# Modulation steps handed out one at a time inside the first filter units, with later norms, in a two-layer mLSTM / Hyena / neighbourhood-attention trunk

## The chip, the core and the metric

One NeuronCore of a Trainium2 chip runs the whole forward pass in one launch. The metric is device time in microseconds; smaller is better. Its engines are named here as the profile names them: PE is TensorE (matrix products; PEld is its weight load), DVE is VectorE, ACT is ScalarE, POOL is GpSimd and SP is SyncE, which issues most transfers. Each engine works off its own instructions strictly in order, and engines wait for one another by semaphores.

## The reference, cut to what matters

A stream of 1024 latent tokens and one of 256 context tokens, 1024 channels wide, pass two layers. Layer 0 mixes an mLSTM (four heads) with a Hyena long convolution; layer 1 is neighbourhood attention with 16 heads. Each layer ends in a squared-ReLU MLP. What the change touches is the start of layer 0: the modulation, the first norm, and the filters of the Hyena, which do not depend on the tokens.

```python
mod_x = (silu_c @ w_mod[l] + b_mod[l])[:, None, :]        # shift, scale, gate
hx = rms_norm(x) * (1.0 + sc1) + sh1
...
h = jnp.sin(freq * (emb @ w1 + b1))
h = jnp.sin(freq * (h @ w2 + b2))
h = (h @ w3).astype(f32).reshape(L, HYENA_ORDER, 2, MIX_B)
h = h * jnp.exp(-t * deltas)[:, None, None, :]
h = h * lax.rsqrt(jnp.sum(h * h, axis=0, keepdims=True) + EPS)
```

Every `rsqrt` of the kernel (the token norms, the norms of q and k in the attention, the norms of the mLSTM heads and of the filters) is computed on ACT as `Exp(-0.5 * Ln(v))` with one Newton step on DVE behind it.

## The kernel before, in words

Tokens stand transposed, 128 channels by 512 tokens to a tile, in three groups (512, 512 and 256 tokens, `GR`). A product of full precision is made of three passes with split operands (L177 to L179 for the projections, L312 to L314 for the second half of the MLP). Program order and priorities go into a scheduler, which writes the final order of each engine; it is that order which the chip runs.

The stages, in order: (1) filters: `filter_hidden` makes the two small sine layers, and nine turns of a loop run `filter_taps` for one of eight units (taps L514 and L515, norm `newton_small` L140 and L141, scaling by the result L525, transposes L532) and `filter_spectrum` for the unit before. Between them the callback `between` places the modulation of layer 0 (`mod_part`, L218) and the norms of the three token groups (`norm_sum` with L252, `rstd_from` with L132 and L133, `norm_apply` with L289); (2) the Hyena blocks with projections as filler, and the gates (`Ln` and `Exp` at L691 and L732); (3) four mLSTM heads (`Ln` and `Exp` at L799 and L800, head norm at L140 and L141, its result transposed at L872); (4) output projection and norm; (5) the MLP of layer 0, with the norm of layer 1 at its end; (6) eight pairs of attention heads, in which `natten_proj` norms two groups of q and three of k (square L900, sum L902, then L904, `Ln` L905, `Exp` L906) while `natten_attn` of the pair before runs (scores L978 and L979, `Exp` L989 and L990, transposes L999, their copies L1001 out of the only buffer `psm`); (7) the output projection, a norm and the second MLP.

ACT evaluates `Sin`, `Ln` and `Exp` from tables, and an instruction ACT_TABLE_LOAD brings in a set of them when the next function is in another set than the one that is loaded. A pass over the finished order puts these loads in; the kernel's own part in it is one line behind the sine layers, at the end of the modulation:

```python
between(-1)
tc.keep_in_program_order(S.preload_act_table_set("natural_log_exp_and_others"))
```

It is L559 before and L563 in the changed kernel. The set that it names holds both `Ln` and `Exp`: in the order before, no load stands behind it, though `Ln` and `Exp` alternate to the end.

Of the kernel before, what the change touches and what calls it, by code (L numbers as in the profile page):

```python
# [17 lines left out]
P = 128  # L18
LAT, CTX, NT = 1024, 256, 1280
# [8 lines left out]
def kernel(ctx: ExitStack, tc: tile.TileContext, A, out):  # L28
    nc = tc.nc
# [9 lines left out]
    def mk(pool, shape, tag, bufs, dt=F32):  # L39
        cnt[0] += 1  # L40
        return pool.tile(shape, dt, tag=tag, bufs=bufs, name=f"{tag}_{cnt[0]}")
# [4 lines left out]
    OR = ((2, 0), (0, 0), (2, 1), (0, 1), (2, 2), (1, 0), (1, 1), (1, 2))  # L46
    E1, E2, E3, E4, E5 = None, None, None, None, None
    NHT, NQ = 1, 2
    NS, NA = (0, 2, 5), {0: (0, 0), 0.5: (0, 8)}
    PN = "n"  # L50
    TA, TB, TC, TV, PO = "m", "m", "m", "m", "f"
    ONP0 = ()
# [23 lines left out]
    def pt(shape, tag):  # L76
        cnt[0] += 1
        return psp[0].tile(shape, F32, tag=tag, bufs=psp[1][tag], name=f"ps{tag}_{cnt[0]}")
# [22 lines left out]
    def sub(o, a, b):  # L101
        return tt(o, a, b, ALU.subtract)

    def mul(o, a, b):
        return tt(o, a, b, ALU.mult)
# [102 lines left out]
    def mod_steps(l, g, pool, bufs, tag):  # L208

        ps = [None]  # L210
        for i in range(16):
            def step(k=i % 8, c0=i // 8 * 256):
                if k == 0 and c0 == 0:
                    ps[0] = pt([P, 512], tag)
                w = mk(pool, [P, 8, P], bufs[0], bufs[1]).rearrange("p (j a) b -> p j (a b)", j=4)
                nc.sync.dma_start(w, A["w_mod"][l, k * P:(k + 1) * P, g * 2048:(g + 1) * 2048].rearrange("p (j c) -> p j c", j=4)[:, :, c0:c0 + 256])
                for j in range(4):
                    T.matmul(ps[0][32 * j:32 * j + 32, c0:c0 + 256], sil[:, k, :], w[:, j], start=(k == 0), stop=(k == 7))  # L218
                if k == 7 and c0:
                    mod_end(l, g, ps[0], tag)  # L220
            yield step

    def mod_part(l, g, pool, bufs, tag="g"):
        for f in mod_steps(l, g, pool, bufs, tag):
            f()
# [268 lines left out]
                sub(st[64:128, t], h[r], st[64:128, t].bitcast(F32))  # L494
        return st

    def filter_taps(qd, o, h2, dec, fa, fp):

        w3 = mk(fa, [64, 256], "w3", 1)
        nc.scalar.dma_start(w3, A["f_w3"][:, o, qd].rearrange("p d c -> p (d c)"))  # L500
        w3h = mk(fa, [P, 256], "w3h", 2, F32R)
        w3l = mk(fa, [P, 256], "w3l", 2, F32R)
        G.memset(w3l[64:128].bitcast(F32), 0.0)
        dsk = mk(fa, [1, P], "dsk", 2)
        nc.scalar.dma_start(dsk, A["hy_d"][:, o, qd])
        S.copy(w3h[0:64], w3)
        S.copy(w3h[64:128], w3)
        sub(w3l[0:64], w3, w3h[0:64].bitcast(F32))
        hT = mk(fp, [P, 2, NT], "hT", NHT)
        ss = mk(fp, [P, 4, 2, 3], "ss", 2)  # L510
        for d in range(2):
            for g, (c0, n) in enumerate(GR):
                ps = pt([P, 512], "t")
                T.matmul(ps[:, :n], w3h[:, d * P:(d + 1) * P], h2[:, c0:c0 + n], start=True, stop=False)  # L514
                T.matmul(ps[:, :n], w3l[:, d * P:(d + 1) * P], h2[:, c0:c0 + n], start=False, stop=True)  # L515
                mul(hT[:, d, c0:c0 + n], ps[:, :n], dec[:, c0:c0 + n])
                sq = mk(fp, [P, 512], "sq", 1)
                S.activation(sq[:, :n], hT[:, d, c0:c0 + n], AF.Square, accum_out=ss[:, 0, d, g:g + 1])
        v, r, tmp = [ss[:, i, :, 0:2] for i in (1, 2, 3)]
        add(ss[:, 0, :, 1:2], ss[:, 0, :, 0:1], ss[:, 0, :, 1:2])  # L520
        V.tensor_scalar(out=v, in0=ss[:, 0, :, 1:3], scalar1=EPS, scalar2=None, op0=ALU.add)
        newton_small(v, r, tmp)
        for d in range(2):
            for l, (a, b) in enumerate(((0, LAT), (LAT, NT))):
                S.activation(hT[:, d, a:b], hT[:, d, a:b], AF.Copy, scale=r[:, d, l:l + 1])  # L525
        hfb = mk(fp, [P, 10, 2, P], "hfb", 2)
        for pr in range(5):
            ps = pt([P, 2, 2, P], "t")
            for i in range(2):
                s = 2 * pr + i  # L530
                for d in range(2):
                    T.transpose(ps[:, i, d], hT[:, d, s * P:(s + 1) * P], ident)  # L532
            S.copy(hfb[:, 2 * pr:2 * pr + 2], ps)
        for s in (0, 8):
            add(hfb[0:1, s, 0], hfb[0:1, s, 0], dsk)
        return hfb
# [14 lines left out]
        X = dft_fwd(mm, fp, False)  # L551
        nc.sync.dma_start(Gd[o, qd], X)

    def filters(hc, Gd, between):
        with tc.tile_pool(name="fa", bufs=1) as fa:
            with tc.tile_pool(name="hid", bufs=1) as hid:
                h2 = filter_hidden(hid, fa)
                between(-1)
                tc.keep_in_program_order(S.preload_act_table_set("natural_log_exp_and_others"))  # L559
            with tc.tile_pool(name="fp", bufs=1, reuse_waits="tile") as fp:  # L560
                last = None
                for u in range(9):
                    if u < 8:  # L563
                        qd, o = divmod(u, 2)
                        if o == 0:
                            dec = mk(fa, [P, NT], "dec", 1)
                            nc.scalar.dma_start(dec, A["dec"][qd])
                        hfb = filter_taps(qd, o, h2, dec, fa, fp)
                        if u == 0:
                            tS = mk(fa, [P, 10, P], "tS", 1)  # L570
                            nc.scalar.dma_start(tS, A["tabF"][:, 2])
                        between(u - 1.5)
                    if last is not None:
                        filter_spectrum(*last, hc, tS, fp, Gd)
                        between(u - 1)
                    last = (qd, o, hfb)
# [447 lines left out]
    Gd = dram([2, 4, P, 2, 10, P])  # L1024
# [30 lines left out]
    with tc.tile_pool(name="hp", bufs=1, side="right") as hp:  # L1055
        hc = {}
        stage = lambda: mk(hp, [P, 512], "st", 1)
        with tc.tile_pool(name="mo", bufs=1, side="right") as mo:

            def xload(t0, n):  # L1060
                t_ = {}

                def f(k):
                    if k % 2 == 0:
                        t_[k // 2] = mk(mo, [P, 2, 512], "wm", 3)
                        nc.sync.dma_start(t_[k // 2][:, :, :n], A["xT"][:, k:k + 2, t0:t0 + n])
                    return t_[k // 2][:, k % 2, :n]
                return f

            norms = {}  # L1070

            def between(u):
                if u == -1:
                    hc.update(hyena_consts(hp))
                    mod_part(0, 0, mo, ("wm", 3), "q")
                for v in NS:
                    g = NS.index(v)
                    t0, n = GR[g]
                    which = 0 if t0 < LAT else 1
                    if u == v:  # L1080
                        norms[g] = norm_sum(xload(t0, n), n, False), xload(t0, n)
                    if u in (v, v + 0.5):
                        r, x = norms[g]
                        norm_apply(r, x, n, 0, 0, which, h[0][g], h[1][g], False, range(0, 8)[slice(*NA[u - v])])
                if u > 4 and u == int(u):
                    filler(FS[u - 5], stage)

            filters(hc, Gd, between)
        open_w()
        psum(**PS1)  # L1090
        with tc.tile_pool(name="wp2", bufs=1, reuse_waits="tile") as wp:
            hc["tI"] = mk(wp, [P, 2, 10, P], "tI", 1)
            nc.scalar.dma_start(hc["tI"], A["tabI"])
            u = decimate(hy_block(0, h, hc, wp), wp)
            for qd in range(4):
                if qd == GQ:
                    gs = gates(h, wp, gk)
                B = hyena_fft(qd, 0, u, hc, wp, Gd)
                if qd == GQ - 0.3:
                    gs = gates(h, wp, gk)  # L1100
                x1 = decimate(hy_block(3 * qd + 1, h, hc, wp), wp)
                x2 = hy_block(3 * qd + 2, h, hc, wp)
                filler(FH[2 * qd], stage)
                z = hyena_gate(qd, 0, B, x1, x2, hc, wp, mixd)
                B = hyena_fft(qd, 1, z, hc, wp, Gd)
                if qd < 3:
                    u = decimate(hy_block(3 * qd + 3, h, hc, wp), wp)
                filler(FH[2 * qd + 1], stage)
                if qd == GQ - 0.5:
                    gs = gates(h, wp, gk)  # L1110
                hyena_gate(qd, 1, B, x1, x2, hc, wp, mixd)
    psum(**PS3)
    with tc.tile_pool(name="gp", bufs=1, reuse_waits="tile", side="right") as gp:
        cst = mlstm_consts(gp)
        with tc.tile_pool(name="ml", bufs=1, reuse_waits="tile") as ml:
            h2 = []
# [68 lines left out]
    with tc.tile_pool(name="nl", bufs=1, reuse_waits="tile") as nl, \  # L1185
# [13 lines left out]
        h2 = new_h(LG)  # L1199
# [168 lines left out]
```

## Time and profile before

| | us |
|---|---|
| three timed runs, median | 3416.87 |
| lowest and highest | 3413.32, 3423.29 |
| the profiled execution's own time | 3412.15 |
| its span in the trace | 3410.4 |
| PE busy | 3256.5 (95%) |
| DVE busy | 2056.0 (60%) |
| ACT busy | 1211.5 (36%) |
| mean granted clock of TensorE | 0.983 of full |

Busy time is summed over the span; an engine with a small share can still be the one that another waits for in some stage. In the rows of the trace a number like 0.63 behind a start time is the duration in us, and what stands in square brackets is how long the engine sat idle before it and what ended that wait.

### The profile page before, as it was taken

To read this page: it belongs to the slowest core of one execution; us is meant where nothing else is said; L and a number is where in the kernel's file an instruction comes from. 1 tells how busy PE (TensorE), PEld (TensorE's weight loads), DVE (VectorE), ACT (ScalarE), POOL (GpSimd) and SP (SyncE) were. 2 spreads that over 40 slices of the span, in tenths; PEclk is the share of its full clock that TensorE was granted. 3 is DMA by queue.
4 is the path that set the end of the run, shared out by engine and by line. 5 is a ranking of instruction groups with operands and counts; after the bars stand their busy time and mean duration, and the time that the engine had idled before them with its cause. 6 is when DMAs were issued, how large, how long until landed. Compare 5 with 4: busy or idle time off the path is not lost.

```text
span 3410.4 us, 45323 instructions
## 1 busy us (share of the span) xinstructions
PE 3256.5 (95%) x18044; PEld 2652.5 (78%) x18044; DVE 2056.0 (60%) x3655; ACT 1211.5 (36%) x2555; POOL 355.8 (10%) x295
## 2 busy tenths in 40 slices
PE   6889989999989999999999999999999899999999
PEld 4777878777877888788888777777777688888887
DVE  4858979366576445444454776666666755545444
ACT  5742222244343121211111476666665421111111
POOL 0341232101120000000000211111110200000000
PEclk8999999999999999999999999999999999999999
DMA  6432211775632121212111212221224211111111
GB/s 210 151 110 66 72 64 64 256 233 198 204 126 87 61 82 56 93 56 87 56 37 38 78 47 72 69 67 62 70 78 161 68 56 47 47 50 47 47 50 68
DMA packets 140878, 306.12 MB, mean 90 GB/s; under 512 B 12497, under 2 KB 74057, under 8 KB 139258
## 3 DMA queue, kind: packets, MB, share of 16 engines
q1 hardware_dynamic: 131018, 266.60, 23.8%
q0 software_dynamic: 6464, 28.84, 2.8%
q10 hardware_dynamic: 3184, 7.78, 0.7%
q8 instruction: 142, 2.33, 0.3%
q14 instruction: 70, 0.57, 0.1%
HBM read 255.93 MB, written 43.05 MB: 88 GB/s over the span
## 4 chain that ended last, share of the span: by engine, by line
PE 64%; DVE 5%; DMA 4%; ACT 3%; issue 1%; POOL 0%; ACTq 0%; SPq 0%; DVEq 0%; POOLq 0%
PE psg L177 10%; PE psg L178 10%; PE psg L179 10%; PE psf L312 8%; PE psf L313 8%; PE psf L314 8%; DMA wm<-in_w_mod 2%; PE psf L1014 2%; PE psm L999 1%; DVE n L108 1%; PE psf L978 1%; PE psf L979 1%; PE psf L1018 1%; PE psm L1006 1%; DVE h L108 1%
## 5 line engine op out<-in xcount | busy, mean ns | idle before, releaser
L177 PE MATMUL psg<-h,wh 128*128 128x512 f32 (+1 forms) x2728 | 1017.6, 373 | 16.7 <-ACT h L289 8.3
L179 PE MATMUL psg<-h,wl 128*128 128x512 f32 (+1 forms) x2728 | 1009.2, 370 | 10.8 <-POOL wl L113 6.0
L178 PE MATMUL psg<-h,wh 128*128 128x512 f32 (+1 forms) x2728 | 1014.8, 372 | 4.2 <-DVE h L108 3.0
L177 PEld LDWEIGHTS psg<-h,wh 128*128 128x128 f32 x2728 | 518.8, 190 | 111.3 <-issue 16.2
L178 PEld LDWEIGHTS psg<-h,wh 128*128 128x128 f32 x2728 | 519.4, 190 | 100.7 <-issue 14.0
L179 PEld LDWEIGHTS psg<-h,wl 128*128 128x128 f32 x2728 | 518.9, 190 | 101.3 <-issue 10.8
L108 DVE SCALAR_TENSOR_TENSOR x<-psf,modT,x 128x512 f32<-128x512 f32 (+1 forms) x512 | 347.4, 683 | 225.6 <-PE psf L314 225.4
L313 PE MATMUL psf<-al,w2h 128*128 128x512 f32 (+1 forms) x1280 | 473.3, 370 | 0.3 <-DVE al L113 0.3
L314 PE MATMUL psf<-ah,w2l 128*128 128x512 f32 (+1 forms) x1280 | 472.2, 369 | 0.0
L312 PE MATMUL psf<-ah,w2h 128*128 128x512 f32 (+1 forms) x1280 | 470.6, 370 | 0.9 <-ACT ah L112 0.8
L112 ACT CAST w2h<-w2r 128x1024 fp32r<-128x1024 f32 x64 | 67.3, 1052 | 765.8 <-PE psf L313 594.8
L312 PEld LDWEIGHTS psf<-ah,w2h 128*128 128x128 f32 x1280 | 241.7, 189 | 44.5 <-ACT ah L112 3.2
L313 PEld LDWEIGHTS psf<-al,w2h 128*128 128x128 f32 x1280 | 242.0, 189 | 42.1 <-DVE al L113 1.4
L314 PEld LDWEIGHTS psf<-ah,w2l 128*128 128x128 f32 x1280 | 242.0, 189 | 41.3 <-issue 1.2
L112 ACT CAST wh<-wr 128x1024 fp32r<-128x1024 f32 (+2 forms) x144 | 148.6, 1032 | 288.1 <-PE psg L178 225.2
L113 DVE TENSOR_TENSOR wl<-wr,wh 128x1024 fp32r<-128x1024 f32 (+1 forms) x105 | 127.5, 1214 | 151.3 <-ACT wh L112 150.9
L108 DVE SCALAR_TENSOR_TENSOR rr<-psg,rr 128x512 f32<-128x512 f32 x160 | 101.4, 634 | 179.6 <-ACT rr L301 179.6
L113 POOL TENSOR_TENSOR wl<-wr,wh 128x1024 fp32r<-128x1024 f32 (+1 forms) x39 | 134.0, 3436 | 607.2 <-ACT wh L112 554.9
L113 DVE TENSOR_TENSOR w2l<-w2r,w2h 128x1024 fp32r<-128x1024 f32 x64 | 78.3, 1223 | 153.1 <-ACT w2h L112 151.3
L301 ACT ACTIVATE rr<-psg 128x512 f32<-128x512 f32 x160 | 88.1, 551 | 196.6 <-PE psg L179 195.3
L112 ACT CAST ah<-rr 128x512 fp32r<-128x512 f32 x160 | 92.4, 578 | 168.1 <-DVE rr L108 168.1
L113 DVE TENSOR_TENSOR al<-rr,ah 128x512 fp32r<-128x512 f32 x160 | 101.8, 637 | 80.5 <-ACT ah L112 80.3
(295 smaller groups left out, 4329.7 us busy)
## 6 DMA issues: line engine op xcount, KB each, us to landing
wm<-in_w_mod SPq DMA_DIRECT2D x96, 512.0 KB
wr<-in_w SPq DMA_DIRECT2D x64, 512.0 KB
w2r<-in_w SPq DMA_DIRECT2D x64, 512.0 KB
big<-d SPq DMA_DIRECT2D x39, 640.0 KB
TM<-in_rpbT POOLq DMA_DIRECT2D x64, 384.0 KB, 3.4
wr<-in_w_in SPq DMA_DIRECT2D x29, 512.0 KB
wr<-in_w_qkv SPq DMA_DIRECT2D x24, 512.0 KB
d<-b SPq DMA_DIRECT2D x8, 1280.0 KB
```

The lines of the kernel that those rows point to most:

```text
L108: return V.scalar_tensor_tensor(out=o, in0=a, scalar=s, in1=b, op0=op0, op1=op1)
L112: S.copy(hi, x)
L113: (e or V).tensor_tensor(out=lo, in0=x, in1=hi.bitcast(F32), op=ALU.subtract)
L177: T.matmul(ps[:M, :n], hi[:, k, :M], hh[g][:, k, :n], start=(i == 0), stop=False)
L178: T.matmul(ps[:M, :n], hi[:, k, :M], hl[g][:, k, :n], start=False, stop=False)
L179: T.matmul(ps[:M, :n], lo[:, k, :M], hh[g][:, k, :n], start=False, stop=(i == len(ks) - 1))
L301: S.activation(r[:, :n], ps[:, :n], AF.Relu)
L312: T.matmul(ps[:, :n], w2h[:, d], ah[g], start=(i == 0), stop=False)
L313: T.matmul(ps[:, :n], w2h[:, d], al[g], start=False, stop=False)
L314: T.matmul(ps[:, :n], w2l[:, d], ah[g], start=False, stop=(i == 1))
L978: T.matmul(o, Q[hh][:, c0:c0 + P], kx, start=True, stop=False)
L1014: T.matmul(po[64 * hh:64 * hh + 64, rb], Vw[:, rb + j, 64 * hh:64 * hh + 64], pT[hh][0][rb][:, j], start=(j == 0), stop=False)
```

## The change

`mod_part` is no longer run in one go at `between(-1)`. Its sixteen steps (one load of 512 KB by SP and four matrix products each) go into a list, and `filter_taps` takes one from it after each of its six products with `h2` and after each of its five transposes. The norms of the first two token groups begin one unit later (`NS`), and before a norm is applied all steps that are left are taken. The ring `wm` has five buffers in place of three. The load of `dec` for the first quarter is issued ahead of the sine layers.

```diff
-    NS, NA = (0, 2, 5), {0: (0, 0), 0.5: (0, 8)}
+    NS, NA = (1, 3, 5), {0: (0, 0), 0.5: (0, 8)}
...
                 S.activation(sq[:, :n], hT[:, d, c0:c0 + n], AF.Square, accum_out=ss[:, 0, d, g:g + 1])
+                tick()
...
             S.copy(hfb[:, 2 * pr:2 * pr + 2], ps)
+            tick()
...
         with tc.tile_pool(name="fa", bufs=1) as fa:
+            dec = mk(fa, [P, NT], "dec", 1)
+            nc.scalar.dma_start(dec, A["dec"][0])
             with tc.tile_pool(name="hid", bufs=1) as hid:
...
-                        t_[k // 2] = mk(mo, [P, 2, 512], "wm", 3)
+                        t_[k // 2] = mk(mo, [P, 2, 512], "wm", 5)
...
+            def tick(n=1):
+                for f in mods[:n]:
+                    f()
+                del mods[:n]
...
                     hc.update(hyena_consts(hp))
-                    mod_part(0, 0, mo, ("wm", 3), "q")
+                    mods.extend(mod_steps(0, 0, mo, ("wm", 5), "q"))
...
                     if u in (v, v + 0.5):
+                        tick(16)
```

What the scheduler makes of it is shown at three places. Lines of the changed kernel are higher by 4 in the attention and by 1 to 10 elsewhere. On PE, at the start of the program, the sixteen steps (L218) stood among the sine layers (L482) and the first taps (L514, L515) already. Before:

```order
L480 MATMUL psf_130<-emb_113,fw_12_115 64x320 x2
L218 MATMUL psq_173<-wm_174,sil 32x256 x4
...
L218 MATMUL psq_173<-wm_198,sil 32x256 x4
L482 MATMUL psf_144<-fh_19_134,fw_13_117 64x320 x2
L482 MATMUL psf_148<-fh_19_134,fw_13_117 64x320 x2
L218 MATMUL psq_173<-wm_204,sil 32x256 x4
...
L218 MATMUL psq_173<-wm_234,sil 32x256 x4
L514 MATMUL pst_301<-h2s_161,w3h_291 128x512
```

And now:

```order
L480 MATMUL psf_132<-emb_115,fw_13_117 64x320 x2
L218 MATMUL psq_198<-wm_199,sil 32x256 x4
...
L218 MATMUL psq_198<-wm_259,sil 32x256 x4
L482 MATMUL psf_146<-fh_20_136,fw_14_119 64x320 x2
L482 MATMUL psf_150<-fh_20_136,fw_14_119 64x320 x2
L218 MATMUL psq_198<-wm_283,sil 32x256 x4
...
L218 MATMUL psq_198<-wm_331,sil 32x256 x4
L218 MATMUL psq_198<-wm_359,sil 32x256
L514 MATMUL pst_192<-h2s_163,w3h_182 128x512
```

Five steps stood ahead of the second sine layer and six stand there now; eleven stood ahead of the first taps, and eleven and a quarter do now. On ACT, the first three dozen rows: where the line of the preload went. Before it stood behind the copy of the finished modulation (L229):

```order
L352 DMA cb_171<-in_conv_b 128x12
L567 DMA dec_287<-in_dec 128x1280
L500 DMA w_50_289<-in_f_w 64x256
...
L456 ACT_TABLE_LOAD
L456 ACTIVATE fh_19_134<-fx_125 128x640
...
L140 ACT_TABLE_LOAD
L140 ACTIVATE ss_300<-ss_300 128x2x2
L229 COPY n_47_270<-psq_173 128x512
L559 ACT_TABLE_LOAD
L141 ACTIVATE ss_300<-ss_300 128x2x2
```

Now it stands ahead of the first sine (L456), whose own load comes after it:

```order
L352 DMA cb_173<-in_conv_b 128x12
L563 ACT_TABLE_LOAD
L500 DMA w_31_180<-in_f_w 64x256
...
L456 ACT_TABLE_LOAD
L456 ACTIVATE fh_20_136<-fx_127 128x640
...
L140 ACT_TABLE_LOAD
L140 ACTIVATE ss_191<-ss_191 128x2x2
L229 COPY n_89_413<-psq_198 128x512
L141 ACT_TABLE_LOAD
L141 ACTIVATE ss_191<-ss_191 128x2x2
```

What was a load by name at L559 is a load ahead of the `Exp` at L141, and from there on each `Ln` and the next `Exp` have a load of their own. The third place is ACT in the attention, at the second of the five norms of a pair of heads, the one at 2125 us of the trace. Before:

```order
L904 ACTIVATE n_3100_17619<-psn_17621,epsc 128x512
L905 ACTIVATE n_3102_17623<-n_3100_17619 128x512
L906 ACTIVATE n_3102_17623<-n_3102_17623 128x512
L1001 COPY s_3046_17369<-psm_17365 128x384
L1001 COPY s_3048_17375<-psm_17371 128x384
```

And now:

```order
L908 ACTIVATE n_3100_17619<-psn_17621,epsc 128x512
L909 ACT_TABLE_LOAD
L909 ACTIVATE n_3102_17623<-n_3100_17619 128x512
L910 ACT_TABLE_LOAD
L910 ACTIVATE n_3102_17623<-n_3102_17623 128x512
L1005 COPY s_3046_17369<-psm_17365 128x384
L1005 COPY s_3048_17375<-psm_17371 128x384
```

Two loads came in and nothing else moved. Over the whole program ACT has 2143 rows before and 2278 now, and 4 table loads before against 139: 12 each at L140 and L141, 11 each at L132 and L133, 40 at L909 and 39 at L910, 4 each at L803 and L804, and one each at L203, L456, L563, L695, L736 and L993. Behind the filters, the gates and the first Hyena blocks the orders of PE, DVE, ACT and POOL are the same but for these loads.

More of the change, by code (lines that the diff above doesn't have):

```diff
@@ L495, in filter_hidden, with filter_taps @@
         return st
-    def filter_taps(qd, o, h2, dec, fa, fp):
+    def filter_taps(qd, o, h2, dec, fa, fp, tick):
         w3 = mk(fa, [64, 256], "w3", 1)
@@ L552, in filter_spectrum, with filters @@
         nc.sync.dma_start(Gd[o, qd], X)
-    def filters(hc, Gd, between):
+    def filters(hc, Gd, between, tick):
         with tc.tile_pool(name="fa", bufs=1) as fa:
+            dec = mk(fa, [P, NT], "dec", 1)
+            nc.scalar.dma_start(dec, A["dec"][0])
             with tc.tile_pool(name="hid", bufs=1) as hid:
@@ L564, in filters @@
                         qd, o = divmod(u, 2)
-                        if o == 0:
+                        if o == 0 and qd:
                             dec = mk(fa, [P, NT], "dec", 1)
                             nc.scalar.dma_start(dec, A["dec"][qd])
-                        hfb = filter_taps(qd, o, h2, dec, fa, fp)
+                        hfb = filter_taps(qd, o, h2, dec, fa, fp, tick)
                         if u == 0:
@@ L1068, in xload @@
                 return f
-            norms = {}
+            norms, mods = {}, []
+            def tick(n=1):
+                for f in mods[:n]:
+                    f()
+                del mods[:n]
             def between(u):
@@ L1086, in between @@
                     filler(FS[u - 5], stage)
-            filters(hc, Gd, between)
+            filters(hc, Gd, between, tick)
         open_w()
```

## Prediction

> **What bounds the kernel now.** I read the page first, then the busy time by stretches, the groups of ACT, and the timelines of the places where a load is added. The page's first part says which engine is full:
>
> ```profile
> PE 3256.5 (95%) x18044; PEld 2652.5 (78%) x18044; DVE 2056.0 (60%) x3655; ACT 1211.5 (36%) x2555; POOL 355.8 (10%) x295
> ```
>
> TensorE (PE) bounds the whole, and ACT is idle for two thirds. But that is a mean. The stretches, with start and end, length, then busy time of PE, PEld, DVE, ACT and POOL, granted clock, DMA share and GB/s, show the start, the filters, the mLSTM heads, the norms ahead of the first MLP, and the attention:
>
> ```profile
> 0.00:50.00 50.00, 27.45 (x164) 9.33 (x165) 16.65 (x40) 21.91 (x41) 1.64 (x9) 0.85 0.85 271
> 42.00:250.00 208.00, 176.83 (x1115) 146.17 (x1116) 140.38 (x304) 133.32 (x290) 66.89 (x63) 0.93 0.40 135
> 640.00:960.00 320.00, 310.21 (x1936) 253.44 (x1935) 193.34 (x451) 130.15 (x394) 38.91 (x18) 0.99 0.63 209
> 960.00:1060.00 100.00, 87.78 (x393) 65.68 (x392) 78.28 (x112) 44.33 (x75) 26.57 (x19) 0.93 0.31 108
> 1975.00:2570.00 595.00, 583.73 (x3827) 456.45 (x3826) 411.23 (x912) 397.45 (x975) 88.51 (x132) 1.00 0.23 71
> ```
>
> In the first 50 us PE idles for 22.55 us; in the filters no engine is full, so a chain through several of them sets the pace; in the attention PE is at 98% and ACT at 67%.
>
> **What the order did with the change.** The steps of the modulation were spread among the sine layers and the first taps before, and they still are, at nearly the same places. What moved in earnest is one line on ACT: the load of the set that holds both `Ln` and `Exp` now runs ahead of the sine, whose own load discards it. From then on each `Ln` and each `Exp` behind it fetches its set: 139 loads where 4 were. One of the new ones (L563) runs ahead of the first sine, where ACT is waiting anyway; 134 others are new. The groups give counts and places, and the load's time:
>
> ```profile
> L132 ACT ACTIVATE n<-n 128x512 f32<-128x512 f32 (+1 forms) x11 | 6.3, 577 | 0.3
> L140 ACT ACTIVATE ss<-ss 128x4 f32<-128x4 f32 (+1 forms) x12 | 2.4, 203 | 3.7 <-DVE ss L521 3.0 <-DVE ss L866 0.7
> L799 ACT ACTIVATE big<-big 128x1280 f32<-128x1280 f32 x4 | 5.1, 1275 | 3.7 <-DVE big L798 3.7
> L905 ACT ACTIVATE n<-n 128x512 f32<-128x512 f32 (+1 forms) x40 | 23.7, 593 | 2.0 <-DVE n L108 1.2
> L140 ACT ACT_TABLE_LOAD x1 | 1.3, 1283 | 0.0
> ```
>
> A load took 1283 ns, so a pair of `Ln` and `Exp` costs ACT 2.57 us more, and all 134 cost 171.9 us. The two loads that before has inside the filters show that nothing else is paid:
>
> ```profile
> 42.85 1.28 ACT L140 ACT_TABLE_LOAD   x1
> 44.14 0.21 ACT L140 ACTIVATE ss<-ss 128x4 f32<-128x4 f32 x1
> 44.26 0.57 ACT L229 COPY n<-psq 128x512 f32<-128x512 f32 x1
> 44.84 1.28 ACT L559 ACT_TABLE_LOAD   x1
> 46.13 0.21 ACT L141 ACTIVATE ss<-ss 128x4 f32<-128x4 f32 x1
> ```
>
> The copy ends at 44.83 and the load starts at 44.84; the next function starts 0.01 us after the load's end. The Trainium skill, ScalarE: Activation LUTs, section "What ACT_TABLE_LOAD costs", gives 1283 ns for the load, which the trace shows, and about 1380 ns for a drain with it, 2.66 us for every switch, which these rows do not show. By that page the 134 would cost ACT 356 us, and the sum at the end, its stalls grown by 2.66 to 1.28, would be near 3725.
>
> **What lies on the path, stage by stage.** Attention first: 80 of the loads (40 at L909, 39 at L910, one at L993), 102.6 us, ten to each of eight pairs of heads. Three of the five norms of one pair of heads, ACT's rows and the PE row that comes next:
>
> ```profile
> 2105.93 0.63 ACT L906 ACTIVATE n<-n 128x512 f32<-128x512 f32 x1
> 2107.25 0.46 ACT L1001 COPY s<-psm 128x384 f32<-128x384 f32 x1
> 2107.76 0.55 PE L999 MATMUL psm<-ident,pe 128*128 128x128 f32 x3
> ...
> 2125.99 0.64 ACT L906 ACTIVATE n<-n 128x512 f32<-128x512 f32 x1
> 2127.25 0.48 ACT L1001 COPY s<-psm 128x384 f32<-128x384 f32 x1 [0.63 <-PE psm L999]
> 2127.79 0.55 PE L999 MATMUL psm<-ident,pe 128*128 128x128 f32 x3
> ...
> 2141.45 0.63 ACT L906 ACTIVATE n<-n 128x512 f32<-128x512 f32 x1
> 2142.75 0.60 ACT L900 ACTIVATE n<-psg 128x512 f32<-128x512 f32 x1 [0.67 <-PE psg L179]
> 2143.55 1.02 PE L902 MATMUL psn<-n,bd 128*128 128x512 f32 x2
> ...
> 2156.26 0.83 ACT L938 CAST KK<-n 64x256 fp32r<-64x256 f32 x2 [1.87 <-DVE n L96]
> 2157.17 0.39 PE L978 MATMUL psf<-KK,Q 128*128 128x256 f32 x1
> ```
>
> The next transposes need the copy, since `psm` is one buffer. In the first case the copy ends at 2107.71, 0.05 ahead of PE, and ACT has hardly a gap between: PE is late by some 2.4 us. In the second ACT has 0.63 of idle and PE a margin of 0.06: 2.57 - 0.69 = 1.9 us. In the first k norm the square L900 waits 0.67, so PE's sum is late by 1.9 again. The other two k norms follow within 12 us, and the last cast ends at 2157.09, 0.08 ahead of the scores L978, behind `Exp`, DVE and cast in a row; of the three pairs' 7.70 us I take 6.4, between 1.9 (the first alone) and 7.0 (all but 0.67). Together 10.7 us of 12.83 to a pair of heads, 86 us to eight; bounds 50 (the three readings alone) and 102.6. PE has no slack to hide it, having idled 11.3 of 595 us.
>
> The filters: eight norms at L140 and L141 and three at L132 and L133 lie there, 22 loads, of which two were paid before: 20, 25.7 us. The second unit shows the chain:
>
> ```profile
> 64.00 0.21 ACT L140 ACTIVATE ss<-ss 128x4 f32<-128x4 f32 x1
> 64.67 0.21 ACT L141 ACTIVATE ss<-ss 128x4 f32<-128x4 f32 x1
> 67.54 2.99 ACT L525 ACTIVATE hT<-hT,ss 128x1024 f32<-128x1024 f32 x4 [2.67 <-DVE ss L108]
> 68.74 0.44 PE L532 MATMUL pst<-ident,hT 128*128 128x128 f32 x2
> ```
>
> The scaling waits for DVE, which needs L141; the transposes follow. I take 22 us, bounds 10 and 25.7. Gates and heads hold 18 loads, 23.1 us. The four head norms are exposed, as PE already waits for their product, while the loads at L803 and L804 lie beside a PE that is 97% busy; I take 9, bounds 0 and 23. The eight norms left (three ahead of each MLP's first products or at layer 0's end, two in layer 1) are 20.5 us; the last of a stage is awaited in full, the others run beside products of another group: 15, bounds 7 and 20.5. The rows for these:
>
> ```profile
> 774.03 0.66 PE L872 MATMUL psm<-ident,big 128*128 128x128 f32 x4 [1.66 <-DVE big L96]
> 1043.92 0.38 PE L177 MATMUL psg<-h,wh 128*128 128x256 f32 x1 [1.61 <-ACT h L289]
> ```
>
> Sum of the loads: 86 + 22 + 9 + 15 = 132 us.
>
> **The clock.** Each such stall can also cost speed afterwards. A stretch of 3.41 us in which PE idled, and the next one; then products at half and at full clock:
>
> ```profile
> 915.95:919.36 3.41, 1.56 (x12) 1.23 (x11) 3.41 (x5) 2.06 (x7) 0.00 (x0) 1.00 0.22 78
> 919.36:922.77 3.41, 3.41 (x14) 3.12 (x14) 3.41 (x6) 1.81 (x5) 0.61 (x1) 0.50 0.56 180
> ```
>
> ```profile
> 2667.16 0.63 PE L177 MATMUL psg<-h,wh 128*128 128x512 f32 x1
> 2670.15 0.52 PE L178 MATMUL psg<-h,wh 128*128 128x512 f32 x1
> 2670.50 0.39 PE L179 MATMUL psg<-h,wl 128*128 128x512 f32 x1
> 2673.03 0.39 PE L178 MATMUL psg<-h,wh 128*128 128x512 f32 x1
> ```
>
> 1.85 us idle in one stretch, and the next has a granted clock of 0.50. From 2667.16 to 2670.15 seven products start, 0.43 us each; from 2670.50 to 2673.03 eleven, 0.23 each. A half-speed stretch thus does 8 products in place of 14.8 and loses 1.6 us. New stalls of 1.8 us or more: four to each of eight pairs of heads, and about 22 elsewhere. One of 1.9 lies within a single stretch in (3.41 - 1.9)/3.41, nearly half, of the cases, one of 2.4 gives 1.85 us to one stretch in about 0.6 of them, the last of the pair always. I count 17 in the attention (one lost time falls into a later stall) and 8 elsewhere: 25 x 1.6 = 40 us, bounds 0 and 54 x 1.6 = 86. The Trainium skill, TensorE: Matmul & The Clock Gate, Part 1, has the clock fall after at least one idle window of about 3.4 us; the row above fell after 1.85. By that page the stalls here would leave the clock alone, and the sum would be 3547 (the first rival).
>
> **The start.** Sixteen loads of 512 KB feed the modulation, and PE waits for them:
>
> ```profile
> PE psq L218 <- DMA wm<-in_w_mod: 16.2, 10, 4.3
> ```
>
> With five buffers the loads queue without gaps; the first row by stretches has DMA at 0.85, so at most 0.15 x 50 = 7.5 us are to be had. But unit 0 hangs on the sine layers, whose second one now stands behind one step more. I take 2 us of gain, between 7 and a loss of 3. SP's queue has the same sixteen loads first; those of `xT` behind them keep their places but for their turn with the stores of the spectra, so the norms that are asked for a unit later start where they did, and the last one was not moved. The load of `dec` that goes ahead on ACT's queue costs nothing, since ACT idles until the first sine layer's products. POOL's order is the same.
>
> **Sum.** The profiled execution's time is 3412.15 us (span 3410.4). 132 + 40 - 2 = 170 gives 3582 us. The median of the runs is 4.7 us above it, so I forecast 3587.
>
> **The rivals.** First, the clock stays: the loads stall PE, but stalls of 1.9 to 4.5 us, cut up by the sequence of other products, do not throttle: 3587 - 40 = 3547 us. For it: PE is busy on both sides of each stall, and the clock answers a stretch's mean. Against it: the row at 915.95. Second, each load costs as much again, since ACT must run empty ahead of it: the stalls double, and nearly every one then fills a stretch (60 us of clock), 3417 + 264 + 60 - 2 = 3739. Against it: the rows at 44.26 to 46.13. This is the drain that the Trainium skill names in the section cited above. Third, the loads are hidden: ACT has 198 us of idle in the attention and needs 103 of it, so if PE's queue ran ahead only the filters would pay, 3417 + 22 - 2 = 3437. Against it: margins of 0.05 and 0.06 us. Fourth, on the other side, faster: the load at L563 serves the whole program, so that `Ln` and `Exp` find what they need and the loads listed are not carried out, and the deeper ring saves 7 us by the DMA's share, or at best the 16.2 us that PE waits for these loads: 3410 to 3401. It decides if the profile after shows four or five loads. Against it: the trace before has the four loads that its order lists, each carried out in 1283 ns.
>
> **Chances.** The forecast 0.62, by itself 3560 to 3645. Clock unmoved 0.24. Drain 0.05. Hidden 0.05. Faster 0.04. The range 3525 to 3645 takes in the first two, with the loads at 108 us and no throttling below, and at 170 us and 60 of throttling above. About 0.3% (10 us) is what a measurement of this kernel tells from no change. Faster 0.03, within it 0.02, slower 0.95.
>
> **What would show it.** Right: 139 ACT_TABLE_LOAD in the groups of ACT at about 1283 ns, ACT busy near 1385 us; the attention, 595 us before, near 708; L999, L902 and L978 waiting 2 us and more behind ACT; granted clock there near 0.96. Wrong: an attention of less than 640 us, or new waits in the filters alone. If the clock stays at 1.00 in the attention, the first rival was right.

## The result and the profile after

The changed kernel took 3584.34 us (median of 6 runs, 3580.29 to 3591.22) where the kernel before took 3418.30 (6 runs, 3413.32 to 3423.96): 1.0486 times as long, with a 95% interval of 1.0473 to 1.0499. The forecast was 3587. The profiled execution took 3585.11 us, with a span of 3583.3 and a mean granted clock of 0.969, where before had 3410.4 and 0.983.

The busy times of the changed kernel, from its page:

```profile
PE 3308.9 (92%) x18044; PEld 2689.1 (75%) x18044; DVE 2052.9 (57%) x3655; ACT 1383.4 (39%) x2690; POOL 339.4 (9%) x295
```

Two things are to be seen. ACT has 171.9 us more than before; the 135 loads that came in are 135 x 1.283 = 173.2 us, so its other work is 1.3 us shorter. And the span splits: it is 172.9 us longer, PE is busy 52.4 us longer with the same 18044 products, and idle 120.5 us longer (3583.3 - 3308.9 against 3410.4 - 3256.5). Idle time is waiting. Products that take longer are products at a lower clock, and the clock's own record agrees: what was not granted is (1 - 0.969) x 3583.3 = 111.1 us against (1 - 0.983) x 3410.4 = 58.0, so 53.1 us more.

The groups of ACT show the loads; 102 of the 139 are in these rows, the others at L133, L141, L803, L804 and six single lines:

```profile
L909 ACT ACT_TABLE_LOAD x40 | 51.3, 1283 | 1.5 <-DVE n L108 0.8
L910 ACT ACT_TABLE_LOAD x39 | 50.0, 1283 | 0.7
L140 ACT ACT_TABLE_LOAD x12 | 15.4, 1283 | 0.3
L132 ACT ACT_TABLE_LOAD x11 | 14.1, 1283 | 0.2
```

To see where the time went, both spans are cut at the same instructions: the last product of the filters, the first of the mLSTM heads, the first of the output projection, the first of the second half of the MLP, the first sum of a q or k norm (L902, now L906), and the last score (L978, now L982). The columns are start and end, length, then busy time of PE, PEld, DVE, ACT and POOL, granted clock, DMA share and GB/s. The kernel before:

```profile
0.00:206.58 206.58, 164.12 (x1091) 126.96 (x1092) 141.99 (x311) 134.24 (x295) 54.46 (x57) 0.93 0.50 165
206.58:637.57 430.99, 382.72 (x2195) 327.59 (x2194) 321.45 (x576) 101.15 (x179) 99.35 (x33) 0.94 0.28 90
637.57:958.27 320.70, 310.91 (x1950) 254.43 (x1948) 192.28 (x449) 130.01 (x394) 38.43 (x17) 0.99 0.64 210
958.27:1008.86 50.59, 43.51 (x196) 33.94 (x194) 39.61 (x55) 24.57 (x38) 16.35 (x9) 0.93 0.51 179
1008.86:1981.29 972.43, 952.58 (x5081) 786.93 (x5081) 503.83 (x749) 218.30 (x356) 40.29 (x34) 0.99 0.20 64
1981.29:2613.58 632.29, 619.18 (x4090) 483.97 (x4091) 441.24 (x986) 418.64 (x1036) 88.36 (x134) 1.00 0.24 76
2613.58:3410.37 796.79, 783.46 (x3449) 638.68 (x3447) 415.65 (x533) 184.55 (x260) 18.51 (x12) 1.00 0.17 58
```

The changed kernel:

```profile
0.00:234.81 234.81, 174.21 (x1092) 131.68 (x1092) 141.46 (x312) 162.28 (x316) 49.51 (x57) 0.90 0.43 143
234.81:664.44 429.63, 383.66 (x2195) 328.34 (x2194) 321.35 (x576) 103.45 (x181) 90.28 (x33) 0.95 0.28 92
664.44:999.18 334.74, 314.05 (x1950) 257.19 (x1948) 189.78 (x449) 150.64 (x410) 38.42 (x17) 0.98 0.60 201
999.18:1052.53 53.35, 44.82 (x197) 35.45 (x195) 39.31 (x55) 26.90 (x40) 15.09 (x9) 0.90 0.48 169
1052.53:2041.61 989.08, 954.63 (x5081) 789.35 (x5082) 503.55 (x749) 231.10 (x366) 40.17 (x34) 0.99 0.20 63
2041.61:2781.68 740.07, 652.15 (x4091) 506.46 (x4091) 441.74 (x985) 519.62 (x1116) 87.98 (x134) 0.95 0.20 65
2781.68:3583.34 801.66, 785.41 (x3449) 640.61 (x3447) 415.69 (x533) 189.39 (x264) 17.96 (x12) 0.99 0.17 57
```

Length less PE busy is PE's idle time. Subtracting row from row gives:

| stage | longer by, us | of it PE idle | of it PE busy |
|---|---|---|---|
| filters | 28.2 | 18.1 | 10.1 |
| Hyena blocks and gates | -1.4 | -2.3 | 0.9 |
| mLSTM heads | 14.0 | 10.9 | 3.1 |
| output projection and norm | 2.8 | 1.5 | 1.3 |
| MLP, norm of layer 1, first q and k | 16.7 | 14.6 | 2.1 |
| attention | 107.8 | 74.8 | 33.0 |
| behind it | 4.9 | 2.9 | 1.9 |

In the attention the waits of PE say for whom it waits (columns: us in total, times, longest). Before:

```profile
PE psm L999 <- ACT s L1001: 4.8, 12, 0.8
...
PE psn L902 <- ACT n L900: 1.1, 4, 0.4
...
PE psf L978 <- DVE KK L96: 0.2, 1, 0.2
```

After:

```profile
PE psm L1003 <- ACT s L1005: 33.8, 25, 2.5
PE psf L982 <- DVE KK L96: 25.3, 7, 4.1
PE psn L906 <- ACT n L904: 19.5, 14, 2.8
```

These are the three places that the prediction named. One of the stalls, in the timeline (start, duration, engine and line):

```profile
2192.36 1.28 ACT L909 ACT_TABLE_LOAD   x1
2193.65 0.63 ACT L909 ACTIVATE n<-n 128x512 f32<-128x512 f32 x1
2194.30 1.28 ACT L910 ACT_TABLE_LOAD   x1
2195.59 0.63 ACT L910 ACTIVATE n<-n 128x512 f32<-128x512 f32 x1
2196.73 0.46 ACT L1005 COPY s<-psm 128x384 f32<-128x384 f32 x1
2197.24 0.55 PE L1003 MATMUL psm<-ident,pe 128*128 128x128 f32 x3 [2.24 <-ACT s L1005]
```

The copy out of the only `psm` buffer stands behind both loads, and PE sat idle for 2.24 us until it was done.

The clock, in stretches of 3.41 us, after one stall that fell into a single stretch, and around the stall just shown, which is cut in two by a stretch's end:

```profile
2117.38:2120.79 3.41, 1.16 (x7) 0.69 (x6) 0.53 (x2) 3.05 (x5) 0.00 (x0) 1.00 0.00 0
2120.79:2124.20 3.41, 3.41 (x22) 2.77 (x21) 0.42 (x1) 0.48 (x1) 0.00 (x0) 0.50 0.00 0
...
2192.47:2195.88 3.41, 2.52 (x13) 1.69 (x11) 1.24 (x5) 3.37 (x4) 0.76 (x1) 1.00 0.34 112
2195.88:2199.30 3.42, 2.06 (x13) 1.59 (x14) 2.94 (x5) 3.28 (x12) 0.00 (x0) 1.00 0.01 4
2199.30:2202.71 3.41, 3.41 (x20) 2.93 (x19) 3.41 (x10) 2.57 (x5) 0.00 (x0) 1.00 0.03 7
```

With 2.25 us idle in one stretch the next has half the clock. With 0.89 in one and 1.36 in the next, the same 2.25 us together, the clock stays at 1.00.

### The profile page after: what moved, and what is told of

The parts are those of the page before. It is cut to its first block, busy times and chain, and to the rows that moved or that the text cites. A ratio compares the mean times of both kernels' runs of the same rounds, so it can differ in the third digit from the quotient of the medians.

```text
span 3583.3 us, 45468 instructions
## 1 busy us (share of the span) xinstructions
PE 3308.9 (92%) x18044; PEld 2689.1 (75%) x18044; DVE 2052.9 (57%) x3655; ACT 1383.4 (39%) x2690; POOL 339.4 (9%) x295
## 4 chain that ended last, share of the span: by engine, by line
PE 52%; ACT 8%; DVE 4%; DMA 3%; issue 2%; POOL 0%; ACTq 0%; DVEq 0%; POOLq 0%
PE psg L177 8%; PE psg L179 8%; PE psg L178 8%; PE psf L312 7%; PE psf L313 7%; PE psf L314 7%; DMA wm<-in_w_mod 3%; ACT L909 1%; DVE n L108 1%; PE psf L1018 1%; PE psf L982 1%; ACT L910 1%; PE psm L1003 1%; PE psf L983 1%; PE psm L218 1%
## 5 line engine op out<-in xcount | busy, mean ns | idle before, releaser
L177 PEld LDWEIGHTS psg<-h,wh 128*128 128x128 f32 x2728 | 525.5, 193 | 125.1 <-issue 16.5
L178 PEld LDWEIGHTS psg<-h,wh 128*128 128x128 f32 x2728 | 525.0, 192 | 100.4 <-issue 14.0
L113 POOL TENSOR_TENSOR wl<-wr,wh 128x1024 fp32r<-128x1024 f32 (+1 forms) x39 | 125.1, 3208 | 628.0 <-ACT wh L112 604.3
```

The source lines that it names most:

```text
L113: (e or V).tensor_tensor(out=lo, in0=x, in1=hi.bitcast(F32), op=ALU.subtract)
L177: T.matmul(ps[:M, :n], hi[:, k, :M], hh[g][:, k, :n], start=(i == 0), stop=False)
L178: T.matmul(ps[:M, :n], hi[:, k, :M], hl[g][:, k, :n], start=False, stop=False)
```

## The experiments

**Theory.** The line of the preload is held behind the ACT instruction that was given ahead of it in the program. Before that was the copy of the finished modulation, behind the sine layers. Now the modulation is only a list at that point, and what stands ahead is the issue of a transfer (L352); so the preload is placed ahead of the sine, whose own load throws the set out. The first experiment's place for it agrees: given behind the sine layers, it ran at 35.23 us, behind the second sine at 32.24. All of the loss is these 134 loads: PE waits for ACT, and each wait that is long enough halves the clock afterwards. **Rivals.** The other parts of the change (steps among the taps, later norms, five buffers, the early `dec`) cost or gain something of their own; or it is the number of loads that counts and not the place of each in ACT's order; or the stalls are right and the loss outside the attention was sized by luck.

**The preload back behind the sine layers, the rest of the change kept.**

```diff
                 h2 = filter_hidden(hid, fa)
-                between(-1)
                 tc.keep_in_program_order(S.preload_act_table_set("natural_log_exp_and_others"))
+                between(-1)
```

> The changed kernel with its preload line put behind the sine layers and ahead of the modulation's list, so that the set of Ln and Exp stays loaded: 3 table loads in all. Theory (the added loads are the whole loss): 3405 to 3425 us, within 0.4% of the kernel before; ACT busy near 1210 us. Rival (the loss is in the steps, the ring of five or the later norms, and the loads are hidden): 3560 us or more.

3418.06 us (12 runs) against 3418.65 for before (17 runs), ratio 0.9999 (0.9988 to 1.0009). Its attention, from the same first sum to the same last score:

```profile
1990.13:2621.03 630.90, 617.23 (x4091) 482.90 (x4091) 441.09 (x986) 418.73 (x1036) 88.13 (x134) 1.00 0.25 77
```

That is before's attention within 1.4 us, with the clock at 1.00. The whole loss is the loads, and the rest of the change together is worth nothing that the runs can tell.

**The kernel before without its preload.**

```diff
                 between(-1)
-                tc.keep_in_program_order(S.preload_act_table_set("natural_log_exp_and_others"))
```

> The kernel before with its preload line taken out and nothing else: 137 table loads, steps, ring and norms as before. Theory: 3575 to 3595 us, like the changed kernel. Rival (the loss is in the rest of the change): 3418 us.

3584.06 us (4 runs), ratio 1.0491 (1.0476 to 1.0506): the changed kernel's time with none of its other edits. There are 138 loads, one more than expected, and those of the norms stand where the changed kernel has them:

```profile
L904 ACT ACT_TABLE_LOAD x40 | 51.3, 1283 | 1.5 <-DVE n L108 0.8
L905 ACT ACT_TABLE_LOAD x39 | 50.0, 1283 | 0.7
```

Its filters and its attention, cut at the same instructions as above:

```profile
0.00:227.91 227.91, 166.54 (x1091) 127.16 (x1092) 141.37 (x311) 160.14 (x315) 54.45 (x57) 0.93 0.46 150
...
2040.06:2784.12 744.06, 654.30 (x4092) 508.93 (x4091) 441.94 (x985) 519.40 (x1116) 87.94 (x134) 0.95 0.21 65
```

So the loads are enough for the loss, and with the run above they are also needed for it.

**The loads in the attention alone.** The kernel of the first experiment, and a preload of a set without `Ln` ahead of the attention, so that the loads start there: 85 more than in that kernel, 80 of them in the attention, four in the two norms behind it, and the preload itself ahead of it.

```diff
+        tc.keep_in_program_order(S.preload_act_table_set("exp_and_others"))
         for hp in range(7):
```

> The kernel of e1 with a load of the Exp set ahead of the attention, so that only the attention (79 loads) and the two last norms (4 loads) alternate. Theory: e1 plus 108 for the attention and 5 for the last norms, 3525 to 3540 us. If each load cost the same wherever it stands: e1 plus 84/135 of the loss, 3520. If the loads of the attention are hidden: e1 plus 5.

3540.20 us (3530.80 to 3549.78, 4 runs), ratio 1.0364 (1.0345 to 1.0383): 122 us over the first experiment. Its attention, in the execution of 3530.80 us:

```profile
1989.92:2726.53 736.61, 650.46 (x4085) 504.01 (x4085) 441.55 (x985) 520.28 (x1116) 87.98 (x134) 0.95 0.21 66
```

105.7 us longer than the first experiment's 630.90, of which PE's busy time is 33.2 and its idle time 72.5, nearly the changed kernel's 33.0 and 74.8. What happened ahead of the attention plays no part in it.

**The loads up to the attention.** The changed kernel, and a preload of the right set ahead of the attention.

```diff
+        tc.keep_in_program_order(S.preload_act_table_set("natural_log_exp_and_others"))
         for hp in range(7):
```

> The changed kernel with a second preload of the set for Ln and Exp ahead of the attention: 55 loads, those in the filters, gates, heads and the norms of layer 0, and none in the attention or behind it. By the terms of the forecast: filters 22, gates and heads 9, six of the eight norms 11, eight stretches of half clock 13, so 55 us over 3418, 3473. Rival (the terms outside the attention were too small, as the parts before and behind it in the trace of the changed kernel let one think): 60 to 70 us, 3478 to 3488. If stalls in one stage make later ones cheaper, less than 45 us, the changed kernel less the run with the loads in the attention alone.

3468.46 us (4 runs, with 56 loads), ratio 1.0150 (1.0137 to 1.0163): 50.4 us over the first experiment, 5 under the forecast's terms, and neither the 60 to 70 nor the less than 45 of the rivals. Its filters and its attention:

```profile
0.00:233.53 233.53, 172.94 (x1091) 131.42 (x1092) 142.18 (x312) 162.21 (x316) 47.99 (x57) 0.90 0.44 144
...
2035.33:2668.03 632.70, 619.85 (x4085) 484.41 (x4085) 441.14 (x985) 418.05 (x1036) 87.69 (x134) 0.99 0.25 76
```

The attention is before's again. The two halves add up: 122.1 + 50.4 = 172.5 us, and the changed kernel is 166.3 over the first experiment; the 6 between lie within the spread of these runs (19 us in the run with the loads in the attention alone).

**One load to each norm.** The kernel of the first experiment, and an explicit load of the set that is already there ahead of each `Ln` of the norms in the attention: 40 loads, known to the scheduler.

```diff
+                tc.keep_in_program_order(S.preload_act_table_set("natural_log_exp_and_others"))
                 S.activation(y[:, :n], v[:, :n], AF.Ln)
```

> The kernel of e1 with one load of the same set, which is not needed, ahead of the Ln of each of the 40 norms in the attention: half the dose of e3, 51 us of ACT. Theory (the margin of 0.6 to 0.7 us at three of five norms is used up first, and stalls of about 1 us leave the clock at 1.00): e1 plus 30 to 40 us. Rival (the loss goes by the count of loads): e1 plus 54. Rival (stalls of 1 us also throttle): e1 plus 60 or more.

3433.64 us, ratio 1.0054 (1.0041 to 1.0067): 15.6 us over the first experiment, so 0.39 us for each load of 1.283. Both expectations were too high, mine of 30 to 40 and the linear one of 54. Its attention, from the first sum to the last score:

```profile
1983.66:2634.55 650.89, 628.17 (x4092) 489.45 (x4090) 441.64 (x986) 467.68 (x1076) 88.08 (x134) 0.99 0.24 74
```

20.0 us longer than the first experiment's, 10.9 of it PE busy with the clock at 0.99, where it was expected to stay at 1.00. By the attention alone a load cost 0.50 us; the rest of this execution was 5.4 us shorter, which the loads do not explain. The loads, though they bring in what is there, are carried out:

```profile
L909 ACT ACT_TABLE_LOAD x40 | 51.3, 1283 | 0.7
```

But here two things differ from the changed kernel: there are half as many loads, and the scheduler knows of them, while the loads of the changed kernel are put into an order that is finished. The next run takes the two apart.

**Two loads to each norm, known to the scheduler.**

```diff
+                tc.keep_in_program_order(S.preload_act_table_set("natural_log_exp_and_others"))
                 S.activation(y[:, :n], v[:, :n], AF.Ln)
+                tc.keep_in_program_order(S.preload_act_table_set("natural_log_exp_and_others"))
                 S.activation(y[:, :n], y[:, :n], AF.Exp, scale=-0.5)
```

> The kernel with the preload behind the sine layers (3418 us), and an explicit load of the set that is already there ahead of each Ln and each Exp of the norms in the attention: 80 loads more, as many and at the same places as in the run with the loads in the attention alone (122 us slower), but known to the scheduler, which puts copies and casts of the pair before between them. Theory (a load costs what stands behind it on ScalarE, and each stall throttles besides): the copies that TensorE waits for go ahead of some of the loads, the chain of each norm still grows by 2.57 us; 50 to 80 us slower than 3418, so 3468 to 3498, with 20 to 40 us of half clock in the attention. Rival (only the number of loads counts, 122 us for 80): 3540. Second rival (one load to a norm cost 15.6 us, so two cost twice that): 3449.

3467.82 us, ratio 1.0146 (1.0133 to 1.0159): 49.8 us over the first experiment, at the lower edge of what the theory gave, far from the 122 that the number of loads would give, and from the 31 of twice the single load. Its attention:

```profile
1986.21:2668.84 682.63, 637.87 (x4091) 494.24 (x4091) 434.15 (x986) 516.95 (x1116) 88.53 (x134) 0.98 0.23 71
```

It is 51.7 us longer than the first experiment's, 31.1 of it PE idle and 20.6 PE busy. ACT is as busy as in the changed kernel (516.95 against 519.62), yet PE idles 44.8 us in place of 87.9. The timeline shows why:

```profile
2092.30 1.28 ACT L911 ACT_TABLE_LOAD   x1
2093.59 0.48 ACT L1007 COPY s<-psm 128x384 f32<-128x384 f32 x1
2093.97 0.63 ACT L912 ACTIVATE n<-n 128x512 f32<-128x512 f32 x1
```

The copy for PE now goes between the load and the `Exp` that needed it. PE's waits for that copy and for the square are small, and a new wait for DVE at the end of the norm leads the list:

```profile
PE psg L177 <- DVE n L96: 13.2, 13, 2.3
...
PE psn L906 <- ACT n L904: 4.6, 9, 1.2
PE psm L1005 <- ACT s L1007: 4.5, 9, 1.3
```

So the cost of a load is what the order puts behind it. The same 80 loads made the attention 105.7 us longer in the finished order and 51.7 here: some 54 us were the order's. The totals, 122 and 49.8, lie 72 apart, but the 122 has the five other loads in it, and its median lies 9 us above the execution that was profiled.

**The steps truly among the first taps.** The kernel of the first experiment, with the first product of each step of the first modulation held behind what was given to PE ahead of it.

```diff
                 for j in range(4):
-                    T.matmul(ps[0][32 * j:32 * j + 32, c0:c0 + 256], sil[:, k, :], w[:, j], start=(k == 0), stop=(k == 7))
+                    m_ = T.matmul(ps[0][32 * j:32 * j + 32, c0:c0 + 256], sil[:, k, :], w[:, j], start=(k == 0), stop=(k == 7))
+                    if j == 0 and l == 0 and g == 0:
+                        tc.keep_in_program_order(m_)
```

> The kernel with the preload behind the sine layers (3418 us), and the first product of each of the sixteen steps held behind what was given to TensorE before it: now no step stands ahead of the second sine layer, and one stands behind each pair of taps, which is what the change says and the scheduler undid. If unit 0 of the filters sets the pace of the start: the second sine layer starts by about 16 us in place of 21 to 25, and the end of the filters comes 3 to 7 us earlier, 3411 to 3415. Rival (the modulation and the norms of the tokens set it, and the steps now wait for the taps and hold up the loads of wm and of the tokens behind them): the norms come 5 to 10 us later, and since the Hyena blocks need all three groups, 0 to 10 us slower, 3418 to 3428.

3411.89 us (12 runs) against 3417.12 for before (17 runs), ratio 0.9983 (0.9972 to 0.9994). The second sine layer and the first taps:

```profile
19.11 2.40 PE L484 MATMUL psf<-fh,fw 64*64 64x320 f32 x8 [12.38 <-ACT fh L458]
29.36 0.79 PE L516 MATMUL pst<-h2s,w3h 128*128 128x512 f32 x1 [7.85 <-DVE h2s L96]
```

They start 2.3 and 4.5 us earlier than before's (21.44 and 33.91), the sine layer 3 us later than expected, and the lead does not last: the filters end at 210.35 us, where before has 206.58 and the first experiment 211.39. The time came out in the expected range, and the reason that was given for it did not show. The Hyena blocks behind the filters take 426.0 us, where before and the first experiment have 431.0 and 430.8, but four runs without this edit have 424.2 to 427.7 there. It is the fastest of the kernels measured, by 0.17% of before; where these 5 us lie stays open, since single executions of this kernel, and of the kernel before, lie up to 15 us apart.

## Why the prediction was right

**The loads.** 139 of them at 1283 ns, and ACT busy 1383.4 us against the 1385 forecast. The second rival, a drain with each load, is out: in the timeline above ACT's next function starts 0.01 us after each load and the second load 0.02 us after the `Ln`, and the 40 loads at L909 have 1.5 us of idle time ahead of them in all. The Trainium skill, ScalarE: Activation LUTs, section "What ACT_TABLE_LOAD costs", gives 1283 ns for the load and about 1380 ns for a drain. The 1283 ns agree, and the drain does not appear in this kernel. By the drain the sum would have been 3417 + 274 + 40 - 2 = 3729; the 3725 of the working is a slip.

**The attention.** Forecast 86 us of stalls and 27 of clock, measured 74.8 and 33.0: 107.8 against 113. The copies cost 33.8 us where before had 4.8, so 29.0 more, 3.6 to a pair of heads, where the working had 2.4 + 1.9 = 4.3. The k norms cost 25.3 + 19.5 = 44.8 where before had 0.2 + 1.1, so 43.5 more, 5.4 to a pair, where it had 6.4. Both were taken too high. The places were those of the working, the single stalls not quite: PE waited for a copy 25 times, 1.4 us on average, where the working had two waits of 2.4 and 1.9 to each of eight pairs.

**The other stalls.** Filters 22 less 2 for the start: 18.1. Gates and heads 9: 10.9 - 2.3 = 8.6. The eight norms left 15: 1.5 + 14.6 + 2.9 = 19.0, within the bounds of 7 to 20.5. Not all of the 14.6 is from the loads named: PE's wait for the weights of the second layer's modulation (L218) grew from 5.9 to 12.1 us in that stage, which the forecast did not have. That growth does not go with the loads: the same wait is 8.6 to 10.2 us in the five experiments without loads in that stage, and 6.6 and 11.1 in the two with them. The kernel before without its preload, where nothing but the loads differs, has 18.9 us more idle time in the filters, 14.7 in gates and heads, 17.7 for the eight norms and 76.7 in the attention. So the 8.6 fits the 9 better than one execution can vouch for.

**The clock.** Forecast 40 us, measured 52.4: 33.0 / 1.6 = 21 half-speed stretches' worth in the attention where 17 were counted, and 19.4 us elsewhere where 13 were. In the kernel before without its preload it is 47.1 us, 35.1 in the attention and 12.0 elsewhere. This term was too small, mostly in the attention, and the first rival (clock unmoved, 3547) is out: 0.95 there. The Trainium skill, TensorE: Matmul & The Clock Gate, Part 1, has the clock fall after at least one idle window of about 3.4 us. The trace differs: the stretch at 2117.38 was idle for 2.25 us of 3.41, and the next one had half the clock.

**The start.** Forecast 2 us of gain, measured a delay at that place. The first step, the second sine layer and the first taps of the changed kernel:

```profile
14.82 1.08 PE L218 MATMUL psq<-wm,sil 128*32 128x256 f32 x8 [8.33 <-DMA wm<-in_w_mod]
...
23.73 2.40 PE L482 MATMUL psf<-fh,fw 64*64 64x320 f32 x8
...
36.64 0.79 PE L514 MATMUL pst<-h2s,w3h 128*128 128x512 f32 x1 [2.29 <-DVE h2s L96]
```

Before these stood at 10.90, 21.44 and 33.91 us. The first step's weights were awaited 8.33 us in place of 4.31, and one step more stood ahead of the sine layer. That wait goes with the change and not with the loads: it is 4.67 us in the kernel before without its preload, and 7.0 to 8.6 in the experiments on the changed kernel that leave the steps where they are. Whether the five buffers or the early `dec` make it, no run tells. The first experiment has such a delay too (second sine layer at 24.82) and takes before's time within 0.1%, so at the end it counts for nothing that can be measured.

The total was nearer than its parts: the stalls came out 10 us below the forecast (120.5 against 130) and the clock 12 above, and these cancelled. So it is partly luck that the forecast was off by only 3 us. Nor does the total speak for the working: 134 loads of 1.283 us, paid in full and with the clock left alone, would have given 3417 + 172 = 3589 as well. What speaks for it is the split into waiting and clock, and the runs in which known loads cost 0.4 to 0.6 us each. The third rival (loads hidden) failed by the margins of 0.05 us that spoke against it, the fourth because the load at L563 serves nothing.

## What to carry to other kernels

When an edit changes the order in which code is given to a scheduler, look first at what is pinned to its neighbours: here a line that nobody touched moved ahead of the sine and cost 166 us, and the edit itself nothing. Count the loads of tables in the order after each edit, and price one not by its own length but by what stands behind it on its engine and by the clock that the stall then takes: 1.2 to 1.4 us each here (166 / 134 and 122 / 85) where the order was finished without them, 0.4 to 0.6 (15.6 / 40 and 49.8 / 80) where it was made with them.

## What the runs showed of the hardware

In the rows above, a stall of 2.25 us halved the clock of the next 3.41 us when it fell into one stretch, and one of 2.24 us left it alone when a stretch's end cut it in two (idle time of 0.89 and 1.36 us). About 30% of the loss (52.4 of 172.9 us) was clock and not waiting, in a kernel whose mean granted clock fell only from 0.983 to 0.969. And loads of a set that was already there still took 1283 ns each.
